# A hand-planned two-layer block: room in the plan for small products, one copy moved from GpSimd to ScalarE, and constants fetched later

## The chip, the cores and the metric

The kernel runs on one core of one Trainium2 chip. The metric is device time of one execution in microseconds, the median of several runs. Engines are named as in the profile: PE is TensorE's matmuls and PEld its weight loads, DVE is VectorE, ACT is ScalarE, POOL is GpSimd, SP is SyncE, which issues DMAs.

## The reference

Two layers act on 16 meta tokens followed by 256 tokens of width 1024, all in fp32. A layer is a mixer and a feed-forward part, each with an RMS norm ahead and a residual sum behind. The mixer multiplies the normed tokens by one wide matrix and feeds three branches: a retention, a gated linear recurrence with a decay for each channel (called hgrn2), and an attention that subtracts two softmaxes. Their outputs are gated, projected and summed:

```
proj = hn @ w_in
o_ret = retention(rq, rk, rv, rg)              # 4 heads
o_hg  = hgrn2(hq, hf, hi, hg, lb)              # 8 heads
o_da  = diff_attention(dq, dk, dv, lam, g)     # 8 heads, w = softmax_0 - lam * softmax_1
y = sum_n sigmoid(mg_n) * (branch_n @ w_branch_n)
h = h + y @ w_out
u = conv3(rms_norm(h) @ w_ffn_in)              # causal, 3 taps, over tokens
h = h + (silu(u_gate) * u_val) @ w_ffn_out
```

After the second layer a last norm follows, and the 256 token rows are returned.

## The kernel before

Activations lie with features on the partitions and the T = 272 tokens on the free axis. The second layer computes only 258 columns where the earlier tokens are no longer needed.

**Large products.** All weights come from HBM as one stream of chunks, eight 128 x 128 tiles (512 KB) each. `_Weights.next` fetches a chunk (`wraw`, 3 buffers, SP's queue), rounds it on ScalarE (`whi`, 4 buffers) and subtracts on VectorE to get the rest (`wlo`, 4 buffers). Activations are split the same way (`xh` and `xl`, `b0hi` and `b0lo`, and so on). A tile's product is then three rounded matmuls into the PSUM tile `main` (lines 939 to 941): high by high, low activations by high weights, high activations by low weights. `main` has two buffers; each is evacuated when its two column tiles are done. The list `ORDER` gives the sequence of column pairs: `hq`, `hf`, `hg`, ... for the projection, `b0` to `b2` for the branches' projections, `wo`, `fi` and `fo` for the rest.

**Small products.** The branches' own matmuls (scores, states, outputs, transposes; tiles such as `ds`, `do`, `wt`, `ho`, `ro`, `px`, `ms`) use four further PSUM banks, two with the tag `bank` and two with `acc`. They are put between large products.

**The order of the work.** Nothing is issued when it is written. Every instruction becomes an `_Op` of a `_Plan`, with an engine, an estimated cost, a due time `key` and its dependences from the tiles that it reads and writes. Due times are counted in microseconds of large products (`clock`). No operation may be placed before the large product that is due `EARLY` = 12 us ahead of its key. `_Plan.order` then plays all engines forward with these costs. An operation is ready when its last input is done, plus a lag between engines (`LAG`, 0.35 us from another engine to TensorE). An operation that opens a tile waits until a buffer of that tag is free, which is `FREE` = 0.3 us after the last use of the one before. At each step the engine that can start first takes the operation that can start first, by key where several can. The result is one fixed order for each engine, and the chip runs each engine in that order with semaphores between them. The costs decide only the order; on the chip every instruction starts when its inputs are there and its engine is free.

**The branches' chains.** The parts of a branch are planned with `behind` and their due times spread by `settle` up to `MARGIN` = 12 us ahead of a mark in `ORDER`. The attention has two halves of four heads (`+daa` and `+dab`), each made of `da_first` (the first queries), two calls of `da_heads` (two heads each) and `da_tail` (the last 16 queries of the four heads).

In `da_heads`, each head's weights `w` (the tile `two_a`) are turned by a transposing DMA, so that they can be multiplied with the values. They are first split into 16-bit words in `two_b`, one part by ScalarE and one by GpSimd; the DMA (`turn`, on SP's queue) writes the result over `w`; ScalarE joins it into `a1` (the tile `wts`), and the product `do` follows. GpSimd also copies two groups of 16 columns of `w` into the tile `dt`, which `da_tail` transposes on TensorE (the product `wt`). At the end the outputs of a half, `da`, are split into `b2hi` and `b2lo` for the branch projection `b2`.

**Start-up.** `h` (the tokens) and the first chunks are fetched first. The norm's scale `rstd` comes from a sum of squares over VectorE and GpSimd, a small product `ms` and two ScalarE steps. The first pairs are multiplied with tokens that lack `rstd`, and it is put in at evacuation; from the fifth pair on (`DEFER`) the tokens are scaled: eight GpSimd products `y = h * rstd` and their split into `xh` and `xl`. Three constant blocks (`small`'s second part, `const`, and `lev` with its byte form `masks`) are fetched on the same SP queue as the weights.

Of the kernel before, what the change touches and what calls it, by code (L numbers as in the profile page):

```python
# [15 lines left out]
AF = mybir.ActivationFunctionType  # L16
# [4 lines left out]
P = 128  # L21
# [3 lines left out]
T = META + SEQ  # L25
# [13 lines left out]
TAIL = T - 2 * P  # L39
# [6 lines left out]
EARLY = 12.0  # L46
# [289 lines left out]
class _Plan:  # L336
# [3 lines left out]
    CROSS = 0.15  # L340
    LAG = {("act", "pe"): 0.35, ("dve", "pe"): 0.35, ("pool", "pe"): 0.35, ("pe", "act"): 0.22, ("pe", "dve"): 0.22, ("pe", "pe"): 0.0, ("sp", "act"): 0.0, ("sp", "dve"): 0.0}
    FREE = 0.3
    SWITCH = 1.3
    SHARED = 0.35

# [96 lines left out]
    def order(self):  # L442

        times, mains = [m.key for m in self.main], set(self.main)
        for op in self.ops:
            i = bisect.bisect_right(times, op.key - EARLY) - 1
            if i >= 0 and op not in mains:
                self.queue(op, self.main[i])
        left = {}
        for op in self.ops:  # L450
            for n in op.tiles:
                left[n] = left.get(n, 0) + 1
        free = {tag: [0.0] * k for tag, k in self.room.items()}
        held, out = set(), []
        engines = {"pe": 0.0, "act": 0.0, "dve": 0.0, "pool": 0.0, "sp": 0.0}
        later = {e: [] for e in engines}
        now = {e: [] for e in engines}
        count = 0
        tables = "le"

        def push(op):
            nonlocal count
            count += 1
            heapq.heappush(later[op.engine], (op.ready, count, op))

        for op in self.ops:
            if op.need == 0:
                push(op)

        def start(op, t):  # L470

            want = {}
            for n in op.tiles:
                if n not in held:
                    want[self.tag[n]] = want.get(self.tag[n], 0) + 1
            first = [o for _, o in now["pe"] if o.count >= self.MANY and o.key < op.key]
            for tag, k in want.items():
                if len(free[tag]) < k + sum(self.tag[n] == tag for o in first for n in o.tiles if n not in held):
                    return None
                t = max(t, sorted(free[tag])[k - 1])  # L480
            return t

        def rank(op):
            late = 8.0 if op.func in self.SETS and self.SETS[op.func] != tables else 0.0
            return op.key + late

        self.end = engines
        self.busy = {e: 0.0 for e in engines}
        taken = shared = 0.0

        def comes(op):
            return op.count < self.MANY or (int(taken) - self.BEGIN.start) % self.PIECE < len(self.BEGIN)

        todo = len(self.ops)
        while len(out) < todo:
            best = None
            for e, t0 in engines.items():
                while later[e] and later[e][0][0] <= t0:
                    _, c, op = heapq.heappop(later[e])
                    now[e].append((c, op))  # L500
                found = None
                for c, op in now[e]:
                    t = start(op, t0) if comes(op) else None
                    if t is not None and (found is None or (t, rank(op), c) < found[:3]):
                        found = (t, rank(op), c, op)
                if later[e]:
                    t1 = later[e][0][0]
                    if found is None or t1 < found[0]:
                        found = (t1, 0.0, -1, None)
                if found is not None and (best is None or found[0] < best[0]):  # L510
                    best = found + (e,)
            if best is None:
                raise RuntimeError("no order: " + str([(e, [o.tiles for _, o in now[e]][:4]) for e in now]))
            t, _, c, op, e = best
            if op is None:
                engines[e] = t
                continue
            now[e].remove((c, op))
            cost = op.cost
            if op.func == "both" and shared > t:  # L520

                cost += min(shared - t, self.SHARED * cost)
            if op.func in self.SETS and self.SETS[op.func] != tables:
                tables = self.SETS[op.func]
                cost += self.SWITCH
                if tables == "le":
                    out.append(None)
                    todo += 1
            for n in op.tiles:
                if n not in held:  # L530
                    held.add(n)
                    f = free[self.tag[n]]
                    f.remove(min(f))
            engines[e] = t + cost
            if op.func == "shared":
                shared = t + cost
            self.busy[e] += cost
            taken += op.count * (1 + self.SEMS)
            done = t + cost + (2.0 if e == "sp" else 0.0)
            for n in op.tiles:  # L540
                left[n] -= 1
                if left[n] == 0:
                    free[self.tag[n]].append(done + self.FREE)
            for o in op.after:
                o.need -= 1
                o.ready = max(o.ready, done + self.LAG.get((e, o.engine), self.CROSS))
                if o.need == 0:
                    push(o)
            if op.run is not None:
                out.append(op)  # L550
            else:
                todo -= 1
        return out
# [11 lines left out]
class _Engine:  # L565
# [5 lines left out]
    def _kind(self, method, args, ins):  # L571

        if method == "activation":
            return args[2]
        if self.name == "pool" and method not in ("memset", "tensor_copy"):
            return "shared"
        if method in ("tensor_tensor", "scalar_tensor_tensor") and not any(x.tensor.name in self.plan.psum for x in ins):
            return "both"

    def __getattr__(self, method):  # L580
        f = getattr(self.engine, method)

        def call(*args, **kw):
# [7 lines left out]
            if self.name == "act":  # L591
                cost += 0.093 * (len(aps) - 2) - (0.043 if ins[0].tensor.name in self.plan.psum else 0.0)
            elif method == "partition_all_reduce":
                cost = 0.5 + 5.9e-3 * n
            elif self.name == "pool" and method == "tensor_copy":
                cost += 0.3
            elif self.name == "pool" and method != "memset":
                cost += 0.75 + 0.7e-3 * n
            if method == "scalar_tensor_tensor":
                cost += 0.06  # L600
            if method == "reciprocal":
# [9 lines left out]
            elif method == "dma_start_transpose":  # L611
                cost = 1.5
# [63 lines left out]
def _trace(ctx, tc, plan, a, depth, probe):  # L676
# [2 lines left out]
    dve = _Engine(plan, nc.vector, "dve", 0.068, 1.042e-3)  # L679
    pe = _Engine(plan, nc.tensor, "pe", 0.0, 4 / 2400)  # L680
    pool = _Engine(plan, nc.gpsimd, "pool", 0.04, 0.85e-3)
    sync = _Engine(plan, nc.sync, "sp", 0.06, 4 / 360e3)
    act_queue = _Engine(plan, nc.scalar, "act", 0.06, 0.0)

    cp = ctx.enter_context(tc.tile_pool(name="cp", bufs=1))
# [60 lines left out]
    for k in range(0, KD, 2):  # L746
        plan.key = -9.0 if k == 0 else 1.4 * k - 7.0
        sync.dma_start(h[:, k : k + 2, :].rearrange("p a t -> p (a t)"), a["h"][:, k * T : (k + 2) * T])
    plan.key = 7.0 + EARLY
    sync.dma_start(small[:, S_LB:], a["small"][:, S_LB:])  # L750
    plan.key = 12.0 + EARLY
    const = fixed([P, C_END], "const")
    sync.dma_start(const, a["const"])
    ident = const[:, C_IDENT : C_IDENT + P]
# [2 lines left out]
    inner = masks[:64, 3 * 64 :]  # L757
    lev_f = slot("levf")[:, : 6 * 64]
    sync.dma_start(lev_f, a["lev"])
    plan.key = 18.0 + EARLY  # L760
    dve.tensor_copy(masks, lev_f)
    plan.key = -5.0

# [279 lines left out]
    for li in range(depth):  # L1043
# [363 lines left out]
        def da_heads(b, heads):  # L1407
# [45 lines left out]
            for a1, sb, hd in zip(a1s, sbs, heads):  # L1453
                w = sb[0]
                src, to = (x[:, : 3 * P].bitcast(U16) for x in (sb[1], w))
                parts = src.rearrange("p (h t) -> p h t", h=2)
                act.activation(parts[:, :, :P], words(w[:, T : T + P]), AF.Copy)
                pool.tensor_copy(parts[:, :, P:], words(w[:, : 2 * P]))
                for g, c in ((0, 2 * P), (1, T + P)):
                    pool.tensor_copy(st[f"dt{b}"][:, g, hd, :], w[:, c : c + TAIL])  # L1460
                turned = turn(to, src)
                act.activation(words(a1[:, META : META + 3 * P]), turned.rearrange("p h n x -> p h (n x)"), AF.Copy)
            for a1, hd in zip(a1s, heads):
# [5 lines left out]
                    act.activation(st[f"do{b}"][:, g, hd, :], o[:, c : c + TAIL], AF.Copy)  # L1469
                dve.tensor_copy(out[:, hd, t0 : 2 * P], o[:, t0 : 2 * P])  # L1470
                sub_norm(out[:, hd, t0 : 2 * P], out[:, hd, t0 : 2 * P])

        def sub_norm(out, o):
            n = o.shape[1]
            r = temp(T, "hr")[:, :n]
            head_rsqrt(r, o, AF.Square)
            stt(out, o, subg[:, li : li + 1], r, MUL, MUL)
# [287 lines left out]
```

## Time and profile before

| | |
|---|---|
| median of 3 runs | 1284.35 us (1283.78 to 1284.60) |
| profiled execution | 1284.63 us |
| its span, first to last instruction | 1282.8 us |
| busy: PE, PEld | 1272.2, 1249.6 us |
| busy: DVE, ACT, POOL | 967.7, 871.6, 186.2 us |
| granted TensorE clock | 0.999 |

In the page's head each engine has its busy time, its share of the span and its count of instructions. A row of windows gives start:end and length, then busy time and instructions of PE, PEld, DVE, ACT and POOL, the clock, the share of the DMA engines and GB/s. A row of waits gives the engine and tile that waited, what ended the wait, the total, how often, and the longest. A row of a timeline gives the start from the span's first instruction, the length, the engine, the line, the operation, output<-inputs with shapes, how many are merged, and in brackets the idle time before it and what ended it. A row for one tile gives the shortest, median and longest duration in ns and the first and last start in us. Nearly everything is on line 617, where the plan's wrapper calls an engine, so tiles tell instructions apart. A row of groups ends in busy time, the mean of one in ns, and the idle time before. A row of DMA issues ends in the size and the median time to landing. In all of them buffer numbers are left out of names.

### The profile page before, as it was taken

What the parts mean: (1) busy time and instruction counts of PE and PEld (TensorE: products, weight loads), DVE (VectorE), ACT (ScalarE), POOL (GpSimd) and SP (SyncE); (2) the same over time, 40 slices, a digit from 0 to 9 for tenths busy, and PEclk for the clock granted to TensorE, in tenths of its full rate; (3) what the DMA queues carried; (4) which work ended last, traced back from release to release, by engine and by line L of the source; (5) the groups of instructions that cost most, each with busy time, mean ns of one, the idle gap of its engine ahead of it and who ended that gap; (6) DMA issues with size and microseconds to landing.
All of it is one profiled execution on the core that took longest, in us unless ns stands there. A gap on an engine that the chain in (4) does not pass through costs nothing.

```text
span 1282.8 us, 26902 instructions
## 1 busy us (share of the span) xinstructions
PE 1272.2 (99%) x10777; PEld 1249.6 (97%) x10777; DVE 967.7 (75%) x1673; ACT 871.6 (68%) x1464; POOL 186.2 (15%) x190
## 2 busy tenths in 40 slices
PE   9999999999999999999999999999999999999998
PEld 9999999999999999999999999999999999999986
DVE  7685788698685789786575858887986867998753
ACT  6877485856787578776456755858567876787743
POOL 4101101213232020000020012012132410200000
PEclk9999999999999999999999999999999999999999
DMA  8665584655756656566556655856467666566663
GB/s 282 186 183 149 171 225 141 148 165 138 217 160 177 181 165 183 179 178 177 174 165 194 182 168 174 215 154 164 151 179 197 165 198 186 160 209 186 198 189 106
DMA packets 98892, 228.41 MB, mean 178 GB/s; under 512 B 45008, under 2 KB 45136, under 8 KB 98768
## 3 DMA queue, kind: packets, MB, share of 16 engines
q1 hardware_dynamic: 98480, 226.18, 60.4%
q8 instruction: 84, 1.38, 0.4%
q10 hardware_dynamic: 288, 0.52, 0.1%
q14 instruction: 40, 0.33, 0.1%
HBM read 216.19 MB, written 1.05 MB: 169 GB/s over the span
## 4 chain that ended last, share of the span: by engine, by line
PE 90%; DVE 5%; ACT 2%; DMA 1%; issue 1%; POOL 0%; SPq 0%; ACTq 0%; DVEq 0%; POOLq 0%
PE main L941 27%; PE main L939 27%; PE main L940 26%; DVE wlo L617 2%; PE fo L1559 2%; PE fo L1561 2%; PE fo L1560 2%; PE do L617 1%; PE ho L617 1%; PE ro L617 1%; PE ds L1427 1%; DMA wraw<-in_w 1%; PE lev L1152 1%; ACT whi L617 1%; DVE two_c L617 0%
## 5 line engine op out<-in xcount | busy, mean ns | idle before, releaser
L939 PE MATMUL main<-xh,whi 128*128 128x272 f32 (+1 forms) x2368 | 686.9, 290 | 0.0
L941 PE MATMUL main<-xh,wlo 128*128 128x272 f32 (+1 forms) x2368 | 679.6, 287 | 0.2 <-DVE wlo L617 0.2
L940 PE MATMUL main<-xl,whi 128*128 128x272 f32 (+1 forms) x2368 | 670.5, 283 | 0.9 <-DVE xl L617 0.9
L617 DVE TENSOR_TENSOR wlo<-wraw,whi 128x1024 fp32r<-128x1024 f32 (+1 forms) x408 | 507.5, 1247 | 214.2 <-ACT whi L617 210.6
L617 ACT ACTIVATE whi<-wraw 128x1024 fp32r<-128x1024 f32 (+1 forms) x408 | 427.3, 1049 | 188.1 <-PE main L940 125.4
L940 PEld LDWEIGHTS main<-xl,whi 128*128 128x128 f32 x2368 | 449.4, 190 | 1.5 <-DVE xl L617 1.1
L939 PEld LDWEIGHTS main<-xh,whi 128*128 128x128 f32 x2368 | 445.7, 188 | 1.4
L941 PEld LDWEIGHTS main<-xh,wlo 128*128 128x128 f32 x2368 | 444.6, 188 | 0.7 <-DVE wlo L617 0.4
L617 POOL PARTITION_ALL_REDUCE hr<-hsq x36 | 74.7, 2092 | 162.1 <-ACT hsq L617 148.6
L617 POOL TENSOR_TENSOR y<-h,rstd 128x272 f32<-128x272 f32 x32 | 39.8, 1275 | 317.0 <-ACT rstd L617 258.7
L617 DVE SCALAR_TENSOR_TENSOR two_b<-u,small,two_b 128x256 f32<-128x256 f32 (+2 forms) x176 | 78.0, 488 | 0.0
L941 PE MATMUL main<-ghi,wlo 128*128 128x272 f32 x176 | 51.0, 290 | 0.0
L939 PE MATMUL main<-ghi,whi 128*128 128x272 f32 x176 | 50.8, 288 | 0.0
L940 PE MATMUL main<-glo,whi 128*128 128x272 f32 x176 | 50.2, 285 | 0.0
L617 ACT ACTIVATE two_b<-u,small 128x272 f32<-128x272 f32 (+1 forms) x88 | 48.3, 597 | 1.6 <-DVE glo L617 1.6
L617 ACT ACTIVATE u<-main 128x544 f32<-128x544 f32 (+1 forms) x40 | 24.4, 610 | 27.4 <-PE main L941 27.4
L939 PE MATMUL main<-b0hi,whi 128*128 128x272 f32 (+1 forms) x128 | 37.1, 290 | 0.0
L939 PE MATMUL main<-b1hi,whi 128*128 128x272 f32 (+1 forms) x128 | 36.9, 288 | 0.0
L617 POOL MEMSET at<- 128x1088 f32 x4 | 4.0, 1008 | 225.9 <-PE far L1152 225.9
L941 PE MATMUL main<-yhi,wlo 128*128 128x272 f32 (+1 forms) x128 | 36.5, 285 | 0.0
L941 PE MATMUL main<-b2hi,wlo 128*128 128x272 f32 (+1 forms) x128 | 36.5, 285 | 0.0
L941 PE MATMUL main<-b1hi,wlo 128*128 128x272 f32 (+1 forms) x128 | 36.5, 285 | 0.0
(263 smaller groups left out, 1989.4 us busy)
## 6 DMA issues: line engine op xcount, KB each, us to landing
wraw<-in_w SPq DMA_DIRECT2D x402, 512.0 KB, 3.6
h<-in_h SPq DMA_DIRECT2D x4, 272.0 KB, 4.8
dec<-in_dec SPq DMA_DIRECT2D x2, 544.0 KB, 4.4
wraw<-in_w SPq DMA_DIRECT2D x4, 256.0 KB, 4.1
const<-in_const SPq DMA_DIRECT2D x1, 937.0 KB, 7.1
gain<-in_gl SPq DMA_DIRECT2D x1, 512.0 KB, 4.5
out<-y ACTq DMA_DIRECT2D x2, 256.0 KB, 2.7
out<-y SPq DMA_DIRECT2D x2, 256.0 KB, 2.7
```

The costliest lines, as they stand in the source:

```text
L617: self.plan.add(self.name, lambda: f(*args, **kw), cost, outs, ins, self._kind(method, args, ins), count)
L939: nc.tensor.matmul(o, wh, hi, start=first, stop=False)
L940: nc.tensor.matmul(o, wh, lo, start=False, stop=False)
L941: nc.tensor.matmul(o, wl, hi, start=False, stop=last)
L1152: nc.tensor.matmul(o, keys, x, start=True, stop=True)
L1427: nc.tensor.matmul(ss[m][:, at : at + nk], q[half, hd, q0 : q0 + P], k[half, hd, :nk], start=True, stop=True)
L1559: nc.tensor.matmul(o, gh, wh, start=False, stop=False)
L1560: nc.tensor.matmul(o, gl, wh, start=False, stop=False)
L1561: nc.tensor.matmul(o, gh, wl, start=False, stop=end)
```

## The change

Five edits; the first three are to the planner's numbers and alter no instruction, only the order.

1. `SLACK` = 0.6 us. A bank of `bank` or `acc` is held for free 0.6 us later, and a TensorE operation that is not a large product is held for ready 0.6 us after an input from another engine would make it so.
2. A transposing DMA is held to take 1.0 us longer.
3. Arithmetic on GpSimd (but not its copies, memsets or all-reduces) costs 0.35 us more in the plan, and a DMA's bytes are priced at 300 instead of 360 GB/s.
4. `small`'s second part, `const`, `lev` and the cast of `masks` are due later: 30, 36, 36 and 44 us instead of 7, 12, 12 and 18, each plus `EARLY`.
5. In `da_heads` one ScalarE copy of 2 x 16 columns of `w` into `dt` replaces two GpSimd copies of 16 columns.

```diff
+    SLACK = 0.6
...
-            done = t + cost + (2.0 if e == "sp" else 0.0)
+            done = t + cost + (2.0 if e == "sp" else 0.0) + (1.0 if op.func == "turn" else 0.0)
             for n in op.tiles:
                 left[n] -= 1
                 if left[n] == 0:
-                    free[self.tag[n]].append(done + self.FREE)
+                    free[self.tag[n]].append(done + self.FREE + (self.SLACK if self.tag[n] in ("bank", "acc") else 0.0))
             for o in op.after:
                 o.need -= 1
-                o.ready = max(o.ready, done + self.LAG.get((e, o.engine), self.CROSS))
+                o.ready = max(o.ready, done + self.LAG.get((e, o.engine), self.CROSS) + (self.SLACK if o.engine == "pe" != e and o not in mains else 0.0))
...
+        if method == "dma_start_transpose":
+            return "turn"
...
             elif self.name == "pool" and method != "memset":
-                cost += 0.75 + 0.7e-3 * n
+                cost += 1.1 + 0.7e-3 * n
...
-    sync = _Engine(plan, nc.sync, "sp", 0.06, 4 / 360e3)
+    sync = _Engine(plan, nc.sync, "sp", 0.06, 4 / 300e3)
...
-    plan.key = 7.0 + EARLY
+    plan.key = 30.0 + EARLY
     sync.dma_start(small[:, S_LB:], a["small"][:, S_LB:])
-    plan.key = 12.0 + EARLY
+    plan.key = 36.0 + EARLY
     const = fixed([P, C_END], "const")
     sync.dma_start(const, a["const"])
...
     sync.dma_start(lev_f, a["lev"])
-    plan.key = 18.0 + EARLY
+    plan.key = 44.0 + EARLY
     dve.tensor_copy(masks, lev_f)
...
                 pool.tensor_copy(parts[:, :, P:], words(w[:, : 2 * P]))
-                for g, c in ((0, 2 * P), (1, T + P)):
-                    pool.tensor_copy(st[f"dt{b}"][:, g, hd, :], w[:, c : c + TAIL])
+                act.activation(st[f"dt{b}"][:, :, hd, :], tails_of(w), AF.Copy)
                 turned = turn(to, src)
...
+        def tails_of(w):
+            return bass.AP(w.tensor, w.offset + 2 * P, [list(w.ap[0]), [T - P, 2], [1, TAIL]])
```

## The prediction

> **What bounds the kernel now.** I read the page's head first, then the groups of instructions, then the waits of TensorE's weight loads, and last the timelines of the first 60 us and of the last attention chain.
>
> ```profile
> span 1282.8 us, 26902 instructions
> PE 1272.2 (99%) x10777; PEld 1249.6 (97%) x10777; DVE 967.7 (75%) x1673; ACT 871.6 (68%) x1464; POOL 186.2 (15%) x190
> PE 90%; DVE 5%; ACT 2%; DMA 1%; issue 1%; POOL 0%; SPq 0%; ACTq 0%; DVEq 0%; POOLq 0%
> 480.00:520.00 40.00, 40.00 (x323) 40.00 (x322) 37.92 (x71) 32.21 (x54) 0.00 (x0) 1.00 0.63 186
> 1080.00:1120.00 40.00, 40.00 (x341) 40.00 (x340) 35.90 (x52) 29.31 (x46) 9.61 (x8) 1.00 0.57 172
> ```
>
> TensorE is the bound: busy 99% of the span and 90% of the chain that ended last. The two windows hold almost only large products: 40/323 = 0.124 us each in the first layer, 40/341 = 0.117 us in the second. The change removes none of them, and no small product either. So all it can win is time in which TensorE stands still because an input or a bank is late. Ends of products are modelled, so a busy TensorE hides short stalls; the waits of its weight loads show them (engine, tile and line, what was waited for: total, times, longest):
>
> ```profile
> PEld wt L617 <- POOL dt L617: 1.9, 2, 1.0
> PEld main L940 <- DVE xl L617: 1.1, 1, 1.1
> PEld warm L617 <- POOL ones_d L617: 1.0, 1, 1.0
> PEld do L617 <- ACT wts L617: 0.8, 2, 0.5
> PEld ho L617 <- PE main L940: 0.7, 1, 0.7
> PEld main L941 <- DVE wlo L617: 0.4, 1, 0.4
> PEld ro L617 <- DVE at L617: 0.4, 1, 0.4
> PEld ms L617 <- DVE sum L617: 0.3, 1, 0.3
> PEld do L617 <- DVE tw L617: 0.2, 1, 0.2
> ```
>
> Without the warm-up's 1.0, which nothing here touches, that is 5.8 us: 4.0 before small products of the branches (wt 1.9, do 0.8 and 0.2, ho 0.7, ro 0.4) and 1.8 in the start-up (xl 1.1, wlo 0.4, ms 0.3). Large products wait nowhere else. Waits under 150 ns are not listed; they bound the sum by perhaps 1 us more. An ideal order would bring about 5.8 of 1284 us, 0.45%. A measurement of this kernel can tell about 0.2%, 2.6 us, from no change: below 1281.8 counts as faster, above 1286.9 as slower.
>
> **The room of 0.6 us.** A small product is put 0.6 us later into TensorE's order than the plan holds its inputs for ready, and a bank is held for free 0.6 us later. The time is not idle: the next large products, whose weights are split well ahead, stand there instead. Of the listed waits before small products only wt (up to 1.0) and ho (0.7) are longer than 0.6. So do and ro go to nothing, ho to 0.1: 2.1 - 0.1 = 2.0 us won. It costs TensorE nothing as long as large products are at hand; without that cover each small product would cost up to 0.6. Bounds: from 0 (every wait comes back elsewhere) to 2.1.
>
> **dt on ScalarE.** The transposes wt wait for GpSimd's copies of the last queries' weights:
>
> ```profile
> L617 POOL COPY dt<-two_a x32: 191/272/2545, 288.5 to 1023.5; 128x16 f32<-128x16 f32 x32
> L617 ACT ACTIVATE qt<-hq 128x32 f32<-128x32 f32 x12 | 2.8, 234 | 0.0
> 1018.47 1.51 POOL L617 COPY dt<-two_a 128x16 f32<-128x16 f32 x2 [7.64 <-DVE two_a L617]
> 1019.92 0.61 POOL L617 COPY two_b<-two_a 128x512 uint16<-128x512 uint16 x1
> 1021.54 2.15 POOL L617 COPY dt<-two_a 128x16 f32<-128x16 f32 x2 [1.01 <-DVE two_a L617]
> 1023.64 0.61 POOL L617 COPY two_b<-two_a 128x512 uint16<-128x512 uint16 x1
> 1018.69 1.20 DVE L617 TENSOR_TENSOR wlo<-wraw,whi 128x1024 fp32r<-128x1024 f32 x1
> ```
>
> A copy of 16 columns takes 0.19 to 2.5 us on GpSimd, and the plan has one price for it; that is why wt came too early. Sixteen ScalarE copies of 32 columns take their place, 0.23 us each by the row of qt: 3.7 us over 16 heads on an engine that is idle 32% of the span. What is queued behind each is the next split of weights or evacuation, 0.23 us later, with several us in hand. The 1.9 us of wt should go whole: bounds 0.9 (late ScalarE, less the room) to 1.9; I take 1.7.
>
> GpSimd's other copy (two_b), which feeds the transposing DMA, stood behind dt: at 1019.92 and 1023.64 instead of, at best, where dt started, 1018.47 and 1021.54. That is 1.5 and 2.1 us sooner, and the attention chain could gain about their mean, 1.8 us, for each pair of heads. But the first dt ended at 1019.98, when VectorE's subtraction wlo had ended at 1019.89: the copy seems to have waited for it. [...]
>
> **The plan's other prices.** The transposing DMA gets 1.0 us more, GpSimd arithmetic 0.35, a DMA byte 1.2 times its price. No instruction becomes slower; the orders of ScalarE and VectorE fit later arrivals. Each queue still does its splits in the gaps: no gain, and a cost only through longer chains (rival below). I take 0; bounds are in the rivals.
>
> **Constants.** small, const and levf move from behind the products of 7, 12 and 12 us to behind those of 30, 36 and 36 us of planned time.
>
> ```profile
> 13.48 0.42 SPq L617 DMA_DIRECT2D small<-in_small  x1
> 16.16 4.29 SPq L617 DMA_DIRECT2D wraw<-in_w  x3
> 20.51 0.42 SPq L617 DMA_DIRECT2D const<-in_const  x1
> 21.42 1.06 ACT L617 ACTIVATE whi<-wraw 128x1024 fp32r<-128x1024 f32 x1 [1.15 <-DMA wraw<-in_w]
> 22.39 0.41 ACT L617 ACTIVATE rstd<-rstd 128x272 f32<-128x272 f32 x1
> 30.41 5.32 POOL L617 TENSOR_TENSOR y<-h,rstd 128x272 f32<-128x272 f32 x4
> 35.03 1.82 DVE L617 SCALAR_TENSOR_TENSOR xl<-y,small,xh 128x272 fp32r<-128x272 f32 x3
> 54.09 1.06 ACT L617 ACTIVATE whi<-wraw 128x1024 fp32r<-128x1024 f32 x1 [1.29 <-PE main L940]
> wraw<-in_w SPq DMA_DIRECT2D x402, 512.0 KB, 3.6
> const<-in_const SPq DMA_DIRECT2D x1, 937.0 KB, 7.1
> small<-in_small SPq DMA_DIRECT2D x1, 441.0 KB, 5.3
> levf<-in_lev SPq DMA_DIRECT2D x1, 192.0 KB, 5.6
> ```
>
> The chunk issued at 16.16 behind small landed just before 21.42, some 5.2 us later where the median is 3.6. ScalarE waited 1.15 us for it with the norm's second step (rstd, 22.39) queued behind; then come eight GpSimd products y, and xl at their end, the 1.1 us wait. With small gone the 1.15 us should go and xl come that much earlier. Against it the plan now holds each y for 0.35 us dearer and may put splits ahead of xl on VectorE. Bounds: 1.1 won to 2 lost; I take 0.6 won, and 0.3 for ms through the room. The wlo wait (0.4) I leave as it is. At their new place the transfers (1570 KB, 3.1 chunks) delay chunks by at most about three chunks' products, 3 x 24 x 0.124 = 8.9 us. By 54 us splits wait for a free buffer, not for a DMA, so the stock covers most of that: I take 0. Two steps of VectorE now follow these transfers closely:
>
> ```profile
> 38.95 0.35 DVE L617 CAST masks<-levf 128x384 uint8<-128x384 f32 x1
> 53.97 0.16 DVE L617 TENSOR_TENSOR p<-small 128x8 f32<-128x8 f32 x1
> ```
>
> const left at 20.51, gated by 12 us of products; 24 us more of them put it near 45, and it lands 7.1 us later, near 52, with levf behind it. The parameters (from 53.97 on) read const, and the cast of masks, moved by 26 us of planned time, reads levf. Behind a late one on VectorE wlo would queue, by 1 or 2 us, which the same stock covers. On SP's queue one or two weight chunks stand behind const.
>
> **Sum.** 2.0 + 1.7 + 0.9 = 4.6 us won; less 0.3 for new short waits of a new order: 4.3. The profiled execution took 1284.63 us (span 1282.8 and 1.83 around it), so 1280.3; the median is 0.28 below it, so 1280.0.
>
> **Rivals.** *All waits go*, the 5.8 and the unlisted ones: about 1278. Only a lucky order does that.
>
> *The waits move.* The order is built anew, and VectorE at 75% leaves the plan's errors as they were. If only wt goes for sure (1.7 won) and the rest comes back: 1282.6. For it: nine waits in 1282 us are already few. Against: the room covers all but two or three of those before small products. That the room changes little, because products wait in the plan for other things, ends here as well.
>
> *The attention chain comes late.* The second half of attention must be split into b2hi and b2lo before the last branch's products use it:
>
> ```profile
> 1041.37 1.23 DVE L617 TENSOR_TENSOR b2lo<-da,b2hi 128x1032 fp32r<-128x1032 f32 x1
> 1043.90 0.28 PE L939 MATMUL main<-b2hi,whi 128*128 128x258 f32 x1
> ```
>
> In the second layer b2lo ends at 1042.6; the first products use the other half, 24 x 0.117 = 2.8 us of them, so it is needed at 1046.7: 4.1 us in hand. The room lengthens the half's chain by six products in series (3.6), two transposing DMAs (2.0) and a bank (0.6): 6.2 us. With the freed copy giving back half of 2 x 1.8 it is 4.4, about what is in hand, and the next group's fed products (2.8 us again) can be put first; I charge nothing. [...]
>
> *Slower* is the same chain at its worst: all ten products of the half pay 0.6 twice and four transposes 1.0 each, 16 us. It decides against the change from 4.1 + 4.3 + 2.6 = 11.0 us on. Half-way, 13.5 us, TensorE waits 9.4 and the time is 1280.0 + 9.4 = 1289.4. For it: nothing paces this chain but itself. Against: the two heads of a pair overlap.
>
> *Constants late*: if the stock covers a third of the 8.9 us, 1280.0 + 5.9 = 1285.9.
>
> **How the numbers follow.** Forecast 1280.0: 0.50. All waits gone, 1278: 0.10. Waits move, 1282.6: 0.15. Lock, 1282.1: 0.09. Constants, 1285.9: 0.03. Chain at its worst, 1289.4: 0.13. Faster is the first two, 0.60; the same, the next three, 0.27; slower 0.13. The range leaves out the slower case and the lower part of the lucky one: 1277.3 to 1286.0.
>
> **What would show it.** Right: the weight loads' wait for dt is gone and no small product waits over 0.3 us; the wait for xl at 35 us is shorter; rstd no longer stands behind a late chunk; b2lo ends 2 to 6 us closer to its products, without a wait. Wrong: a wait of large products for b2hi or b2lo near 1046, for wlo near 45 us, or for xl beyond 1.1; or as many short waits as before in other places.

## The result: 4.4 us faster, from other places than forecast

| | before | after |
|---|---|---|
| median of 6 runs | 1284.47 us (1283.78 to 1285.35) | 1280.04 us (1279.52 to 1281.13) |
| profiled execution, span | 1284.63, 1282.8 us | 1280.53, 1278.7 us |
| ratio to before, 95% interval | | 0.9966 (0.9953 to 0.9979) |

The median lies 0.04 us from the forecast, and the span is 4.1 us shorter where 4.3 had been worked out. The page of the changed kernel begins with its span, busy times and instructions; every line number is 3 higher than before (617 is 620, 939 to 941 are 942 to 944).

```profile
span 1278.7 us, 26891 instructions
PE 1270.1 (99%) x10777; PEld 1248.9 (98%) x10777; DVE 966.7 (76%) x1673; ACT 863.9 (68%) x1474; POOL 173.2 (14%) x158
```

TensorE's count is the same and its weight loads are as busy as they were (1249.6 before): what went is idle time. ScalarE's count shows that the planner's numbers do change some instructions: it is 10 higher, though dt gave ScalarE 16 copies, because a new order needs fewer loads of its function tables (25 instead of 31, 1.28 us each). No run separates what that is worth. The waits of the weight loads, whole:

```profile
PEld main L944 <- DVE wlo L620: 2.3, 4, 1.2
PEld warm L620 <- POOL ones_d L620: 1.0, 1, 1.0
PEld main L942 <- ACT whi L620: 0.4, 1, 0.4
PEld ho L620 <- issue: 0.3, 1, 0.3
PEld wt L620 <- issue: 0.3, 1, 0.3
PEld lev L1155 <- issue: 0.2, 1, 0.2
```

Before small products 0.8 us are left of 4.0, none longer than 0.3. The waits for wts, tw and at are gone, as is that for dt; the rows of ho, wt and lev that stay name no engine. In the start-up, though, 2.7 stands where 1.8 stood: xl and ms are gone, wlo grew from 0.4 to 2.3.

How much each stage won is read more surely from when a given large product starts, in the two timelines: the first product of the thirteenth chunk, the first that reads b2hi in each layer, and the first of the second layer. The same number of TensorE instructions stands ahead of each of these marks in both kernels.

```profile
45.04 0.29 PE L939 MATMUL main<-xh,whi 128*128 128x272 f32 x1
409.96 0.29 PE L939 MATMUL main<-b2hi,whi 128*128 128x272 f32 x1
655.67 0.28 PE L939 MATMUL main<-xh,whi 128*128 128x258 f32 x1
```

```profile
45.57 0.29 PE L942 MATMUL main<-xh,whi 128*128 128x272 f32 x1
408.43 0.29 PE L942 MATMUL main<-b2hi,whi 128*128 128x272 f32 x1
654.15 0.28 PE L942 MATMUL main<-xh,whi 128*128 128x258 f32 x1
1039.84 0.29 PE L942 MATMUL main<-b2hi,whi 128*128 128x258 f32 x1
```

The first fence is the kernel before (its fourth row, 1043.90, stands in the prediction), the second the changed one. To 45 us the change **lost** 0.53 us. From there to b2 in the first layer it won (409.96 - 45.04) - (408.43 - 45.57) = 2.06, and in the second (1043.90 - 655.67) - (1039.84 - 654.15) = 2.54. The feed-forward stretches came out alike. So 4.6 - 0.5 = 4.1. The forecast had the start-up win 0.9 and the branches 3.4 (2.0 + 1.7 - 0.3): two errors of over 1 us with opposite signs.

The windows of these two stretches, before and after, show how much of the 4.6 is idle time of the weight loads (length less PEld's busy time):

```profile
45.04:409.96 364.92, 363.57 (x3246) 358.19 (x3245) 276.52 (x548) 257.26 (x462) 68.53 (x68) 1.00 0.61 172
655.67:1043.90 388.23, 387.09 (x3535) 382.54 (x3533) 297.49 (x556) 266.88 (x484) 79.91 (x83) 1.00 0.63 177
45.57:408.43 362.86, 362.57 (x3245) 358.03 (x3244) 275.63 (x547) 248.07 (x463) 65.69 (x51) 1.00 0.59 175
654.15:1039.84 385.69, 385.69 (x3535) 382.08 (x3533) 295.50 (x555) 268.20 (x491) 70.28 (x66) 1.00 0.60 178
```

It fell from 6.7 + 5.7 = 12.4 to 4.8 + 3.6 = 8.4 us, by 4.0. The listed waits fell by 3.2, so some 0.8 of it lies in waits too short for the list.

The start-up, in the kernel before and then in the changed one, by ScalarE's second and third split of a weight chunk and the 33rd large product:

```profile
5.97 0.61 ACT L617 ACTIVATE whi<-wraw 128x512 fp32r<-128x512 f32 x1
7.96 0.62 ACT L617 ACTIVATE whi<-wraw 128x512 fp32r<-128x512 f32 x1
10.33 0.28 PE L941 MATMUL main<-xh,wlo 128*128 128x272 f32 x1
```

```profile
7.30 0.63 ACT L620 ACTIVATE whi<-wraw 128x512 fp32r<-128x512 f32 x1 [1.22 <-DMA wraw<-in_w]
8.82 0.64 ACT L620 ACTIVATE two_c<-h 128x544 f32<-128x544 f32 x1
9.37 1.13 ACT L620 ACTIVATE whi<-wraw 128x512 fp32r<-128x512 f32 x2
12.35 0.29 PE L944 MATMUL main<-xh,wlo 128*128 128x272 f32 x1
20.49 0.43 ACT L620 ACTIVATE rstd<-rstd 128x272 f32<-128x272 f32 x1
```

What the forecast wanted is there: small leaves at 37.53 instead of 13.48, rstd comes at 20.49 instead of 22.39, the xl that was waited for ends at 34.95 instead of 36.03, and its wait is gone. The experiments show that another edit brought this about. And the loss had come earlier: by 12 us the products are 2.0 us late. ScalarE waits 1.22 us for the second chunk, for which it did not wait before, and its sums of squares (two_c above) now stand ahead of splits (whi) that they stood behind. The cast of masks, now at 55.41, waits 0.82 us for levf on VectorE, and nothing large waits behind it.

The attention's copies, by the changed kernel's rows of the tiles dt and two_b:

```profile
L620 ACT ACTIVATE dt<-two_a x16: 212/214/249, 291.8 to 1022.4; 128x32 f32<-128x32 f32 x16
L620 POOL COPY two_b<-two_a x16: 613/1276/3890, 291.2 to 1022.2; 128x512 uint16<-128x512 uint16 x16
```

Its timeline at the last pair of heads, and where the half of attention is ready:

```profile
1022.19 1.49 POOL L620 COPY two_b<-two_a 128x512 uint16<-128x512 uint16 x1 [2.44 <-DVE two_a L620]
1021.99 1.22 DVE L620 TENSOR_TENSOR wlo<-wraw,whi 128x1024 fp32r<-128x1024 f32 x1
1042.76 1.22 DVE L620 TENSOR_TENSOR b2lo<-da,b2hi 128x1032 fp32r<-128x1032 f32 x1
```

The group of two_b's copies after:

```profile
L620 POOL COPY two_b<-two_a 128x512 uint16<-128x512 uint16 x16 | 23.1, 1446 | 81.3 <-DVE two_a L620 48.6 <-issue 32.7
```

And the groups of the kernel before:

```profile
L617 POOL COPY dt<-two_a 128x16 f32<-128x16 f32 x32 | 21.8, 691 | 66.1 <-DVE two_a L617 66.0
L617 POOL COPY two_b<-two_a 128x512 uint16<-128x512 uint16 x16 | 11.9, 745 | 0.0
```

The mean of a two_b copy went from 745 to 1446 ns: without dt ahead of it, it starts while VectorE subtracts, and the one at 1022.19 ended 0.47 us after the subtraction that had begun at 1021.99. Still, dt and two_b together took 33.7 us over 16 heads and two_b now takes 23.1, so 0.66 us a head came back: even at 1446 ns a two_b copy takes less than two copies of dt and one of two_b did (2.11 us a head).

b2lo now ends at 1043.98, 4.1 us behind the first product of b2; before, it ended 1.3 us ahead of it. So it came 5.4 us closer. The other half's 24 products end 2.8 us after 1039.84, at 1042.6; there is no wait because the plan put fed products of the next group first. The 4.1 us in hand are used up. In the first layer, of which the prediction has nothing, b2lo came closer still:

```profile
401.58 1.28 DVE L617 TENSOR_TENSOR b2lo<-da,b2hi 128x1088 fp32r<-128x1088 f32 x1
409.95 1.29 DVE L620 TENSOR_TENSOR b2lo<-da,b2hi 128x1088 fp32r<-128x1088 f32 x1 [1.45 <-ACT b2hi L620]
```

It ends 2.8 us behind the first product of b2 (408.43) instead of 7.1 us ahead of it (409.96), 9.9 us closer, and still without a wait.

### The profile page after: what moved, and what is told of

The parts are those of the page before. It is cut to its first block, busy times and chain, and to the rows that moved or that the text cites. A ratio compares the mean times of both kernels' runs of the same rounds, so it can differ in the third digit from the quotient of the medians.

```text
span 1278.7 us, 26891 instructions
## 1 busy us (share of the span) xinstructions
PE 1270.1 (99%) x10777; PEld 1248.9 (98%) x10777; DVE 966.7 (76%) x1673; ACT 863.9 (68%) x1474; POOL 173.2 (14%) x158
## 4 chain that ended last, share of the span: by engine, by line
PE 95%; DVE 2%; ACT 1%; issue 1%; DMA 1%; SPq 0%
PE main L944 28%; PE main L942 28%; PE main L943 28%; PE fo L1565 2%; PE fo L1567 2%; PE fo L1566 2%; PE ds L1430 1%; PE do L620 1%; PE ro L620 1%; PE ho L620 1%; PE lev L1155 1%; DVE wlo L620 1%; PE s L620 0%; DVE two_c L620 0%; DMA h<-in_h 0%
## 5 line engine op out<-in xcount | busy, mean ns | idle before, releaser
L620 POOL PARTITION_ALL_REDUCE hr<-hsq x36 | 72.0, 2024 | 170.5 <-ACT hsq L620 155.0
L944 PE MATMUL main<-b0hi,wlo 128*128 128x272 f32 (+1 forms) x128 | 36.5, 285 | 0.0
```

What stands on the lines that cost most here:

```text
L620: self.plan.add(self.name, lambda: f(*args, **kw), cost, outs, ins, self._kind(method, args, ins), count)
L944: nc.tensor.matmul(o, wl, hi, start=False, stop=last)
```

## The experiments

All were timed in five rounds against the kernel before on the same chip. "Won" below is one minus the ratio, times the median of before there (1284.85 to 1285.36 us); by that measure the change itself won 4.4 us (2.7 to 6.0). Each interval reaches about 1.1 us to either side, and the plain difference of medians lies up to 1.0 us away (2.8 us won for the DMA byte's price below, where the ratio gives 1.8), so values less than a microsecond apart are not told apart. Positions in TensorE's order are those of the 1609 small products among the large ones, compared with the changed kernel's, or with the kernel before's for a kernel built on that.

**The changed kernel without the room.**

```diff
-    SLACK = 0.6
+    SLACK = 0.0
```

> The changed kernel with the room set to 0; everything else of the change stays. Theory: the room wins the waits before do, ho and ro, about 2 to 2.5 us with those under the list's threshold; without it they come back, 1282 to 1282.7, while wt stays free of waits because dt is still copied by ScalarE. Rival (the moved constants carry the gain): 1280, no waits of small products come back. Rival (a new order is a lucky draw, no part carries it): anything between 1278 and 1286, with waits at other places.

1284.00 us, ratio 0.9991 (0.9982 to 1.0000): won 1.2, so 3.2 of the 4.4 are gone. The longest of the weight loads' waits before small products:

```profile
PEld ds L1430 <- ACT am L620: 1.1, 1, 1.1
PEld ro L620 <- DVE at L620: 0.9, 2, 0.6
PEld do L620 <- issue: 0.4, 2, 0.2
```

Waits of the kind that the forecast gave to the room are back, with one in a new place (ds), and wt has none, as the theory of dt wants. More is lost than the 2.0 forecast, and the time lies above the range expected. As 967 small products stood elsewhere, a poorer draw among orders is not excluded as part of it.

**dt back on GpSimd.**

```diff
-                act.activation(st[f"dt{b}"][:, :, hd, :], tails_of(w), AF.Copy)
+                for g, c in ((0, 2 * P), (1, T + P)):
+                    pool.tensor_copy(st[f"dt{b}"][:, g, hd, :], w[:, c : c + TAIL])
```

> The changed kernel with dt copied by GpSimd again. Theory: the copies still take up to 2.5 us at one planned price, the room covers 0.6 of it, so the two long waits of wt come back with 0.3 to 0.4 us each and the time is 1280.5 to 1281. GpSimd's other copy is late again and b2lo of the second layer ends 1 to 2 us later. Rival (the copy on ScalarE is what matters, the room is not needed): 1282, wt waits 1.9 us.

1282.70 us, ratio 0.9983 (0.9974 to 0.9991): won 2.2. The rival's number, not the theory's. The room does not cover GpSimd's long copies:

```profile
PEld wt L620 <- POOL dt L620: 1.2, 2, 0.8
PEld do L620 <- ACT wts L620: 0.8, 1, 0.8
```

Both rows are the cost that was forecast for dt: wt itself, and two_b late behind dt. The second can be followed: two copies of dt take 2.82 us from 954.24 on, ahead of two_b; the transposing DMA leaves SP's queue at 957.77 (955.03 in the changed kernel); ScalarE waits for it, then 1.73 us for the weight chunk behind it on that queue, and starts the wts of this do at 967.31 (964.61). Only 92 small products stood elsewhere, so little else can have moved.

**Constants as early as before.**

```diff
-    plan.key = 30.0 + EARLY        # and 36.0, 44.0
+    plan.key = 7.0 + EARLY         # and 12.0, 18.0
```

> The changed kernel with the three constant blocks due as before. The changed kernel lost about 0.5 us in the start-up (first product of the thirteenth chunk at 45.57 instead of 45.04 us) although the wait for xl went. Theory: the constants are not what costs or wins there, the new prices are; early constants bring the 1 us wait for xl back and nothing else: 1280.5 to 1281. Rival (the moved constants carry the whole gain): 1283 to 1284.5.

1280.67 us, ratio 0.9964 (0.9951 to 0.9976): won 4.6, in the range expected. TensorE's order is the same to the last small product. But no wait for xl returns, though small leaves at 14.96: rstd's second step comes at 19.90, and moving the constants is not what made it early. The thirteenth chunk starts at 44.98 instead of 45.57. That is not the constants' work either: the 33rd product already starts at 11.73 instead of 12.35, before small leaves the queue and with the same order on every engine. ScalarE did not wait for the second chunk here, so this is scatter of the first transfers. The 0.6 us is gone again by b1 (355.72 against 355.69).

**All other prices as before** (the transposing DMA, GpSimd's arithmetic, a DMA's byte).

```diff
-            done = t + cost + (2.0 if e == "sp" else 0.0) + (1.0 if op.func == "turn" else 0.0)
+            done = t + cost + (2.0 if e == "sp" else 0.0)
...
-                cost += 1.1 + 0.7e-3 * n
+                cost += 0.75 + 0.7e-3 * n
...
-    sync = _Engine(plan, nc.sync, "sp", 0.06, 4 / 300e3)
+    sync = _Engine(plan, nc.sync, "sp", 0.06, 4 / 360e3)
```

> The changed kernel with the three prices as before (transposing DMA, GpSimd arithmetic, DMA bytes); room, dt and constants stay. Theory: the new prices reorder ScalarE and VectorE in the first 17 us and cost the 2.3 us of waits for wlo there against 0.4 before; with the old prices 1 to 1.5 us come back, 1278.5 to 1279, the transposing DMA's price counting for nothing. Rival (the start-up is no worse than the scatter of the first transfers): 1280. Rival (the transposing DMA's price takes waits of do away): 1281, with waits before do.

1283.60 us, ratio 0.9984 (0.9975 to 0.9993): won 2.1. A miss. The start-up was as expected (thirteenth chunk at 44.63, 0.9 earlier), but the branches lost far more:

```profile
PEld wt L620 <- issue: 1.2, 2, 0.7
PEld ho L620 <- issue: 1.2, 2, 1.0
PEld do L620 <- issue: 0.7, 1, 0.7
```

604 small products stood elsewhere. Where the row says "issue", the wait stands on a semaphore instruction of TensorE's own, ahead of the weight load (in the changed kernel's trace at 262.81 us, ahead of ho at 262.89, and at 280.55, ahead of wt at 280.62); here, for ho at 262.8 us it ended just behind VectorE's `ho<-ho,hr`, the last reading of the bank's earlier tile, at 262.70 in that timeline. Prices that "alter no instruction" were worth 2.3 us, where the forecast took 0.

**Each price by itself.** First only the DMA's byte (the last pair of lines above):

> The changed kernel with only the DMA price per byte as before. Taking back all three prices cost about 3.5 us (four waits for banks and inputs came back) and won 0.9 in the start-up. Theory: each price moves the order where its operation stands, and the DMA price concerns the start-up alone, where its share of the 0.9 would come back: 1279.5 to 1280, no new waits of small products. Rival (any new order scatters by some us, whatever price is changed): 1278 to 1284, with waits of small products somewhere.

1282.53 us, ratio 0.9986 (0.9975 to 0.9997): won 1.8, a miss; 314 small products moved. Its profiled execution lies 3.6 us above its median, so its waits in the branches are not read. The start-up is, because it sorts all fourteen kernels of this document by this one price. In the four with 360 GB/s (this one, the one with all prices back, the kernel before, and the room alone) rstd's second step starts at 21.9 to 23.9 us and xl is waited for by 0.2 to 1.1 us, wherever the constants stand; the 33rd product starts at 10.3 to 11.0. In the ten with 300 or 330 GB/s the sums stand ahead of the splits, rstd's step starts at 19.6 to 20.6, xl is waited for by 0.4 at most, and the 33rd product starts at 11.4 to 12.5. So the price of the DMA's byte, not the constants, brought rstd forward, and it delayed the first chunks' splits. Then only the transposing DMA (the first pair):

> The changed kernel with only the transposing DMA's price as before. Theory: this price is what keeps the waits of do, wt and ho away, because everything behind a transposing DMA (joining the words, do) was planned 1 us early; 1282.5 to 1283.5, waits before do in the attention stages, start-up as in the changed kernel. Rival (the room alone covers that): 1280.

1283.23 us, ratio 0.9984 (0.9975 to 0.9993): won 2.1, in the range expected, but with the waits elsewhere: ho 1.3, lev 0.9, wt 0.8, px 0.8, not do. 614 moved. Then only GpSimd's arithmetic (the middle pair):

> The changed kernel with only GpSimd's arithmetic priced as before. It is used only in the norms. Theory: the dearer price put the splits wlo of the first chunks behind the tokens' split and costs the start-up 0.9 us; 1279 to 1279.5, the branches' small products without waits as in the changed kernel. Rival (scatter of new orders): 1278 to 1284, with waits in the branches.

1280.77 us, ratio 0.9966 (0.9954 to 0.9978): won 4.4, a miss. TensorE's order is unchanged. The thirteenth chunk starts at 44.65, 0.9 us sooner, as the theory wants; but the cause is not this price. To 25 us every engine has the same order as in the changed kernel, and the 33rd product already starts at 11.40 instead of 12.35: again ScalarE did not wait for the second chunk. And b2 starts at 1039.96, no earlier than in the changed kernel:

```profile
PEld ds L620 <- issue: 0.7, 1, 0.7
PEld wt L620 <- issue: 0.5, 1, 0.5
PEld main L943 <- DVE b2lo L620: 0.3, 1, 0.3
```

As with the constants, what the start-up gained was handed back in waits behind it: 1.7 us here, with 0.2 for lev, where the changed kernel has 0.8. TensorE came sooner and its inputs did not. That is why the start-up's error cost the forecast nothing.

**The room alone, on the kernel before.**

```diff
+    SLACK = 0.6
...
-                    free[self.tag[n]].append(done + self.FREE)
+                    free[self.tag[n]].append(done + self.FREE + (self.SLACK if self.tag[n] in ("bank", "acc") else 0.0))
...
-                o.ready = max(o.ready, done + self.LAG.get((e, o.engine), self.CROSS))
+                o.ready = max(o.ready, done + self.LAG.get((e, o.engine), self.CROSS) + (self.SLACK if o.engine == "pe" != e and o not in mains else 0.0))
```

> The kernel before with the room of 0.6 us alone. Theory (parts add up): the waits of do, ho and ro go, those of wt shrink by 0.6 each to 0.4 and 0.3; about 3 us won against the kernel before, 1281.5 to 1282. Rival (the room works only with the dearer transposing DMA and dt on ScalarE): within 1 us of the kernel before, with waits before do and wt.

1284.39 us, ratio 0.9994 (0.9985 to 1.0003): won 0.8, and no difference is not excluded. The rival holds. The room was there, and waits longer than it stood in new places:

```profile
PEld wt L620 <- issue: 1.6, 2, 0.9
PEld wt L620 <- POOL dt L620: 1.0, 1, 1.0
PEld ho L620 <- issue: 1.0, 1, 1.0
PEld do L620 <- ACT wts L620: 0.7, 1, 0.7
```

So the parts do not add. Taken out of the changed kernel one at a time, the room, dt and the prices cost 3.2, 2.2 and 2.3, 7.7 together out of 4.4. The reading that fits is that the room pays only where the plan is otherwise right to within its 0.6 us, which dt on GpSimd (up to 2.5 us where the plan holds one price) and late transposing DMAs broke; the rows that name no engine do not prove it. One more pair can be compared: the kernel with all prices back is this one with dt on ScalarE and late constants, with 55 small products elsewhere, and it won 2.1 where this one won 0.8.

**Other sizes of the room, and an edit without meaning.** Is the changed order itself a lucky draw? Three sizes of `SLACK` in the changed kernel, and in the kernel before a DMA byte priced at 330 instead of 360 GB/s:

```diff
-    SLACK = 0.6
+    SLACK = 0.5        # then 0.7, then 1.2
```

> The changed kernel with a room of 0.5 instead of 0.6 us. Theory (each part covers the plan's errors by its size): a wait of over 0.5 us that 0.6 covered grows by at most 0.1, and few do; 1280 to 1280.8. Rival (the changed kernel's order is a lucky draw; any new order falls back to the level of the experiments that took one part away): 1282 to 1284, with two to four waits of 0.5 to 2 us before wt, do, ho or ds.

1281.36 us, ratio 0.9970 (0.9959 to 0.9981): won 3.9, a miss between the theory's range and the rival's. 192 small products moved, and waits of wt (0.7), ds (0.4) and ho (0.3) are listed.

> The changed kernel with a room of 0.7 instead of 0.6 us. Theory: the same or a little better than the changed kernel, 1279.5 to 1280.5. Rival (lucky draw): 1282 to 1284, with waits as for 0.5 us.

1282.04 us, ratio 0.9973 (0.9963 to 0.9983): won 3.5, a miss: the time is the rival's, but not by the rival's waits. Small products wait 0.6 us in all, but the large ones wait for the second half of attention, whose b2lo began at 1045.77: 1.1 us for b2lo and 0.4 for b2hi.

> The changed kernel with a room of 1.2 us. If more room only covers more: 1279 to 1280, no wait of small products over 0.15 us. The prediction's rival of the late attention chain: in the second layer the chain grows by another 3.6 us or more (b2lo ended at 1044.0 and its product stood ready to wait from about 1042.6, other products placed ahead), so the products of b2 or of the output wait 2 to 4 us: 1282 to 1284. Lucky draw: 1282 to 1284 with waits before wt, do, ho or ds.

1297.58 us, ratio 1.0094 (1.0080 to 1.0108): 12.1 us slower than before. No small product waits over 0.15 us. The list has two waits of the last branch's products instead; the windows hold the stretch behind the stall in each layer (start:end and length; PE, PEld, DVE, ACT and POOL; clock, DMA share, GB/s):

```profile
PEld main L942 <- ACT b2hi L620: 11.0, 2, 6.7
PEld main L943 <- DVE b2lo L620: 2.3, 2, 1.4
```

```profile
418.30:424.00 5.70, 4.64 (x21) 4.34 (x22) 1.53 (x2) 0.00 (x0) 0.00 (x0) 0.57 0.55 184
1059.40:1066.00 6.60, 5.92 (x30) 5.62 (x31) 1.56 (x2) 0.52 (x1) 0.00 (x0) 0.58 0.28 89
```

This is the prediction's slower rival made real, in both layers: 13.3 us of waits for b2hi and b2lo. Most of the rest of the 17.1 by which the span exceeds the changed kernel's is the clock: at a granted 0.57 and 0.58 the next 15 and 20 products started over 3.3 and 4.2 us (419.89 to 423.23 and 1060.62 to 1064.87), where 0.124 and 0.117 each would make 1.9 and 2.3, so 1.5 and 1.9 more.

```diff
-    sync = _Engine(plan, nc.sync, "sp", 0.06, 4 / 360e3)
+    sync = _Engine(plan, nc.sync, "sp", 0.06, 4 / 330e3)
```

> The kernel before with the DMA price per byte at 330 instead of 360 GB/s and nothing else: an edit that means nothing for the small products. Theory: the order of before is typical of a plan without room; within 1.5 us of the kernel before, waits before wt, do, ho and ro of 3 to 5 us in all. Rival (the kernel before was an unlucky draw): 2 to 4 us faster than it.

1287.46 us, ratio 1.0020 (1.0011 to 1.0029): 2.6 us slower than before, with 72 small products moved. That is neither the theory's number nor the rival's, and gives no sign that the kernel before was an unlucky draw. wt waits 2.7 us instead of 1.9, ho 1.5 instead of 0.7, wlo 2.3 instead of 0.4. A price that serves no purpose moves this kernel by more than half of what the whole change did. In the start-up it does what the change did: small leaves at 15.42, as early as the constants' old place gives, yet rstd's second step starts at 20.25, xl is not waited for, and the 33rd product starts at 12.19.

## Why the prediction came out right, and where its steps were wrong

**Right in mechanism and size.** TensorE's idle time before small products was most of what there was to win: the listed 4.0 us became 0.8, and the span shrank by 4.1 with the same matmuls. dt: 1.7 forecast; undoing it alone costs 2.2 and brings back 1.2 for wt and 0.8 for do. two_b: 0.9 us back for each pair of heads was taken; 0.66 a head of GpSimd's time came back, by copies twice as long. b2lo of the second layer came 5.4 us closer, where 4.4 had been worked out with half of the 1.8 us of each pair given back, and 6.2 if nothing is. The rival at 1282.1 (lock, 0.09) stands for a freed copy that gives the chain nothing back, which no run shows: the runs showed the 0.66 us a head, the 5.4 us and no wait of a product for b2lo. The small products' longest wait is 0.3, as named.

**The closeness of the total is luck.** The terms are off by 1.4 us one way and 1.2 the other. In part the two are one: in the two runs with TensorE's order unchanged, a start-up that was 0.6 and 0.9 us sooner left the spans at 1278.8 and 1279.1 against 1278.7, because the branches won that much less.

**The constants and the start-up, wrong.** 0.9 won was forecast and 0.5 lost. The step that failed is "with small gone the 1.15 us should go and xl come that much earlier". With the constants late and the DMA byte at its old price, xl is still waited for by 0.2 and 1.0 us; with the constants early and the new price it is not. What brought rstd forward 1.9 us is the DMA byte's price, by another order on ScalarE, and the same order puts the sums of squares ahead of the first splits, so that the 33rd product starts 2.0 us late. The prediction remarked only that the plan "may put splits ahead of xl". Part of those 2.0 us is scatter: with the same order the 33rd product started anywhere from 11.40 to 12.46 us, by when the second chunk arrived among other things. How the 0.5 us divides is open, and it does not matter to the end, since the branches hand it back.

**"Other prices: 0", mis-sized.** All three undone together cost 2.3 us. Undone alone, the transposing DMA's costs 2.3 and the DMA byte's 2.6 (less by the medians), GpSimd's nothing; these do not add either. The reason given, that no instruction becomes slower, is true and beside the point: a price decides where a product is put, as the room does.

**The branches, low by 1.2.** 3.4 forecast, 4.6 measured. With the start-up as punctual as before (the run with early constants, 44.98) they won 4.0 by the same marks, so 0.6 of the 1.2 is the late start-up's other side. Of the 4.6, 3.2 are listed waits and some 0.8 idle time too short for the list, which the prediction bounded by "perhaps 1 us". The last 0.6 is no idle time of the weight loads, and its cause is open.

**The room priced as a part by itself, 2.0, has no such value.** It is 0.8 alone and 3.2 on top of the rest.

**The attention chain.** Charged nothing, and it cost nothing, by the way out that the prediction named (the next group's fed products first). But it was close: in the first layer b2lo ended only 0.2 us before the other half's 24 products (408.43 + 24 x 0.124 = 411.4); with 0.7 us of room the chain costs 1.5 us, with 1.2 it costs 13.3, and the slower clock 3.4 more (1.5 + 1.9). The prediction bounded the worst chain by 16 us at 0.6; at 0.6 the most that b2lo came closer is 9.9.

**Still open.** How much of the 4.4 us is the edits' own work and how much a good draw among orders is only bounded. Two neighbours with all five edits won 3.9 and 3.5, which speaks for most of it being real; but the intervals are over 1 us wide to each side, and an idle edit moved the kernel before by 2.6 us. The moved copy alone and the constants alone on the kernel before were not tried. No version beat the changed kernel by more than can be measured (4.6 and 4.4 won against 4.4).

## What to carry to other kernels

In a hand-planned static order, sort the tensor engine's waits by stage and by what is waited for, and measure stages by when the same product starts in both kernels; a right total says nothing about its terms. Margins, prices and moved copies act together, so undo each one from the finished version rather than add up what each would bring, and try the neighbours of a tuned number: here 0.1 us more of it brought the next bottleneck, and an idle change of a price 2.6 us. Before a difference between two runs is put down to an edit, find where they first part, and see whether the edit had changed the order by then. A margin given to every step of a chain lengthens the chain by that margin times its number of steps, so work out first how much the longest chain has in hand.

## What the runs showed of the hardware that had not been expected

**Stalls of 4.3 and 6.7 us cost the clock as well.** In the run with 1.2 us of room, products behind the first stall started 0.227 us apart, and 0.124 again some 3 us later:

```profile
420.28 0.43 PE L944 MATMUL main<-b2hi,wlo 128*128 128x272 f32 x1
420.51 0.43 PE L942 MATMUL main<-b2hi,whi 128*128 128x272 f32 x1
423.50 0.29 PE L944 MATMUL main<-b2hi,wlo 128*128 128x272 f32 x1
423.63 0.29 PE L942 MATMUL main<-b2hi,whi 128*128 128x272 f32 x1
```

The windows above show granted clocks of 0.57 and 0.58 there. So a wait of 4.3 and one of 6.7 us cost 1.5 and 1.9 us more than themselves, while the profiled executions of the other kernels, with waits of up to 1.9 us, have a granted clock of 0.999 over the whole span (0.994 here). The slower starts lasted 3.3 us in the first layer (419.89 to 423.23) and 4.2 in the second (1060.62 to 1064.87).

**A small GpSimd copy beside VectorE can take many times its shortest time** (191 to 2545 ns for 16 columns, 613 to 3890 ns for 512 words), where ScalarE's copy of 32 columns stayed within 212 to 249 ns. Of the sixteen copies of 512 words in the changed kernel, five took 0.61 us. The other eleven took 1.0 to 3.9 us beside a VectorE instruction that reads two SBUF tiles (wlo, y or two_c), and ended 0.47 to 0.51 us behind the end of one; the longest lasted through four such instructions in a row. One price in a plan does not cover that width.
